# A hybrid diffusion backbone's mixers: ScalarE's background work behind the last traced eviction, longer runs of small matmuls, two-pass time steps

## The chip, the core and the metric

The kernel runs on one core of one Trainium2 chip. The metric is device time in microseconds (us), the median over runs. TensorE (PE in the rows) does the matmuls, VectorE (DVE) and ScalarE (ACT) the element-wise work; both of these read the matmul results from PSUM, which has eight banks.

## The reference

Two layers over 256 latent tokens and 256 context tokens of width 1024, in fp32. Each layer runs three token mixers on the same normalised input (a bidirectional state-space scan, "SSD", with a short convolution ahead of it; neighbourhood attention; a Conformer convolution of 31 taps), merges them by sigmoid gates, projects by `w_o`, and then runs a SwiGLU (dense in layer 0, a mixture of experts in layer 1).

```
def token_mixer(h_lat, h_ctx, lp, need_ctx):
    ...
    xs_l, bm_l, cm_l = ssd_prepare(h_lat @ w_xbc, lp['ssd_conv_w'], lp['ssd_conv_b'])
    ...
    y_lf, _ = ssd_direction(xs_l, bm_l, cm_l, h_lat @ w_dtf, a_log[0], dt_bias[0], st_f, False)
    ...
    ssd_l = ssd_output(y_lf, y_lb, xs_l, h_lat @ w_z, lp['ssd_d'], lp['ssd_norm'], lp['ssd_out'])
    ...
    na_l = na_latent(heads(h_lat @ w_q), heads(h_lat @ w_k), heads(h_lat @ w_v), k_c, v_c, lp['na_rpb']) @ lp['na_out']
    conf_l = conformer_branch(h_lat @ w_glu, lp['conf_conv_w'], lp['conf_conv_b'], lp['conf_ln_g'], lp['conf_ln_b'], lp['conf_out'])
    out_l = merge_branches(h_lat @ w_gate, (ssd_l, na_l, conf_l)) @ lp['w_o']
```

The SSD works in chunks of 128 tokens: `scores` of C and B, times a decay `exp` of differences of a running sum, times the inputs scaled by the time step `dt` (the within-chunk part), plus C times the incoming state, scaled by `exp(cs)` (the part across chunks). The shift, scale and gate of the norms (`ada`) are products of the conditioning vector with `ada_w`.

## The kernel before

**Projections.** `wstat` (weights stationary, L205 to L207) and `wmov` (L251 to L253) run all projections. Weights come in units of 512 KB. ScalarE rounds a unit to a high part `h_...` (L116), VectorE subtracts it from the raw values to get the low part `l_...` (L117), and each product is three matmuls: high by high, high by low, low by high. Each chunk of 512 output columns uses four of PSUM's banks ("acc"), and each bank is read out ("evicted") by ScalarE or VectorE when its sum is complete. The gates' evictions are sigmoids on ScalarE (`g<-wg`, L682), the short convolution's are copies into `uL` followed by five taps on VectorE (L572) and a SiLU (L560).

**Background work.** Beside the projections run jobs, written as Python generators: `att` (attention: scores `S` L750 and L770, softmax, transposes `PT` L740, values `po` L786), `ssd` (states `stS` L954, decay tiles `MS` by four Relus and an Exp on ScalarE, L1054 and L1055, then a product on VectorE, L1056; within-chunk sums `ydS` L1063; parts across chunks `yoS` L1080 scaled by `ES`, L1077), `conv` (31 taps on `ccv`, then a layer norm and a SiLU L830) and `ada` (sums `adac` on VectorE L374, then column sums on TensorE L382). `pump` is called behind each group of products and takes steps from every job until its credit is used; a step's `yield` is its price. Small matmuls are put off by one or two steps (`defer`), and `behind` ties them to the last large matmul written so far: on TensorE they stand behind it. They write to the other four banks of PSUM ("pw"). Other engines are not tied in this way: a scheduler sets the order on ScalarE and VectorE by priority, program order and what is ready.

**Order of the mixers.** Layer 0: `glu dt qkv xbc ssd g1 p1 g2 p2 z g0 p0`; layer 1 has `z` ahead of `p2`. `g1`, `g2`, `g0` are the gates, `p2` is the Conformer's projection (`wb0conf_out`), `p1` attention's (`wb0na_out`). The time steps are 24 matmuls of `wdtH` and `wdtL` with 32 columns each (L865 to L867) and four small transposes.

## Time and profile before

| | us |
|---|---|
| median of three runs (2364.26 to 2365.93) | 2364.38 |
| the profiled execution | 2367.87 |
| its span, from the first instruction to the last | 2366.1 |
| layer 0's mixers, about | 30 to 690 |
| the dense FFN | 690 to 1010 |
| layer 1's mixers, about | 1095 to 1515 |
| the experts | 1560 to 2366 |

Times in the rows are from the span's start. A row of the timeline gives start, length, engine, line, operation, output and inputs, tile shape, and how many records were merged; a matmul of plain fp32 leaves two records. Matmuls overlap in the pipeline, so the distance between two starts is what one costs, not its length. `128*64` is the shape of the part of the array that is used: two matmuls on different halves run together.

### The profile page before, as it was taken

To read this page: it belongs to the slowest core of one execution; us is meant where nothing else is said; L and a number is where in the kernel's file an instruction comes from. 1 tells how busy PE (TensorE), PEld (TensorE's weight loads), DVE (VectorE), ACT (ScalarE), POOL (GpSimd) and SP (SyncE) were. 2 spreads that over 40 slices of the span, in tenths; PEclk is the share of its full clock that TensorE was granted. 3 is DMA by queue.
4 is the path that set the end of the run, shared out by engine and by line. 5 is a ranking of instruction groups with operands and counts; after the bars stand their busy time and mean duration, and the time that the engine had idled before them with its cause. 6 is when DMAs were issued, how large, how long until landed. Compare 5 with 4: busy or idle time off the path is not lost.

```text
span 2366.1 us, 29723 instructions
## 1 busy us (share of the span) xinstructions
PE 2226.4 (94%) x11075; PEld 1632.5 (69%) x11075; DVE 1509.5 (64%) x2384; ACT 1030.1 (44%) x1658; POOL 17.4 (1%) x32
## 2 busy tenths in 40 slices
PE   7999999699999999999999889899999989999897
PEld 3776677477777777788877779766655656566564
DVE  3667999787667665536898765743433555565556
ACT  4334673643342222225347685443332345454453
POOL 0000000000000000000000000000000000000000
PEclk9999999899999999999999999999999999999998
DMA  7232253445445556423423344488888899999995
GB/s 269 95 117 72 76 172 127 116 156 169 147 143 160 173 175 199 147 98 102 147 89 104 107 146 161 139 324 330 341 320 320 330 365 375 357 385 347 348 370 206
DMA packets 123658, 492.51 MB, mean 208 GB/s; under 512 B 12784, under 2 KB 23792, under 8 KB 89712
## 3 DMA queue, kind: packets, MB, share of 16 engines
q1 hardware_dynamic: 122656, 487.89, 57.4%
q10 hardware_dynamic: 848, 2.62, 0.3%
q8 instruction: 89, 1.46, 0.2%
q14 instruction: 65, 0.53, 0.1%
HBM read 488.24 MB, written 2.23 MB: 207 GB/s over the span
## 4 chain that ended last, share of the span: by engine, by line
PE 71%; issue 11%; DVE 7%; DMA 6%; ACT 4%; POOL 0%; SPq 0%; POOLq 0%; DVEq 0%; ACTq 0%
PE er L1546 8%; PE nn L1428 7%; PE e L1546 4%; DMA adaw<-in_ada_w_dram 4%; PE ndn L1453 4%; PE edr L1546 3%; PE ed L1546 2%; PE wg L205 2%; PE wg L207 2%; PE wg L206 2%; DVE adac L374 2%; PE xbcL L205 1%; PE xbcL L206 1%; PE xbcL L207 1%; PE fu L206 1%
## 5 line engine op out<-in xcount | busy, mean ns | idle before, releaser
L374 DVE SCALAR_TENSOR_TENSOR adac<-adaw,sc,adac 128x512 f32<-128x512 f32 x224 | 160.1, 747 | 57.3 <-DMA adaw<-in_ada_w_dram 56.7
L117 DVE TENSOR_TENSOR l_er<-r_er,h_er 128x1024 fp32r<-128x1024 f32 x132 | 154.5, 1218 | 59.9 <-ACT h_er L116 59.5
L1428 PE MATMUL nn<-r_ngun,xn 128*64 128x512 f32 (+1 forms) x768 | 168.2, 561 | 0.0
L116 ACT ACTIVATE h_er<-r_er 128x1024 fp32r<-128x1024 f32 x132 | 133.0, 1053 | 42.2 <-DMA r_er<-in_moe_gu_dram 29.4
L205 PE MATMUL wg<-hHm,h_wg 128*128 128x512 f32 (+1 forms) x384 | 135.7, 355 | 1.8 <-ACT g L682 1.1
L206 PE MATMUL wg<-hLm,h_wg 128*128 128x512 f32 (+1 forms) x384 | 129.9, 339 | 0.0
L207 PE MATMUL wg<-hHm,l_wg 128*128 128x512 f32 (+1 forms) x384 | 128.8, 339 | 0.5 <-DVE l_wg L117 0.4
L1546 PE MATMUL er<-h_er,gHp 128*128 128x512 f32 (+1 forms) x288 | 110.5, 389 | 17.7 <-ACT h_er L116 17.7
L1428 PEld LDWEIGHTS nn<-r_ngun,xn 128*64 128x64 f32 x768 | 54.2, 137 | 91.9 <-issue 85.1
L1546 PE MATMUL er<-h_er,gLp 128*128 128x512 f32 (+1 forms) x288 | 108.1, 381 | 0.0
L117 DVE TENSOR_TENSOR l_e<-r_e,h_e 128x1024 fp32r<-128x1024 f32 x44 | 52.2, 1222 | 63.5 <-ACT h_e L116 62.6
L1453 PE MATMUL ndn<-r_ndn,hnn 128*64 128x512 f32 x352 | 87.4, 598 | 0.0
L572 DVE SCALAR_TENSOR_TENSOR ccv<-cu,cols,ccv 128x488 f32<-128x488 f32 (+14 forms) x120 | 84.5, 729 | 1.0
L1443 DVE TENSOR_TENSOR hnn<-npn,nsn 128x256 f32<-128x256 f32 (+1 forms) x24 | 9.6, 401 | 117.6 <-ACT nsn L1441 117.6
L1433 ACT ACTIVATE ntn<-nn 128x512 f32<-128x512 f32 (+1 forms) x24 | 13.5, 561 | 162.7 <-PE nn L1428 162.7
L1546 PE MATMUL er<-l_er,gHp 128*128 128x512 f32 (+1 forms) x288 | 84.3, 381 | 0.0
L205 PEld LDWEIGHTS wg<-hHm,h_wg 128*128 128x128 f32 x384 | 72.7, 189 | 14.5 <-issue 4.0
L1546 PEld LDWEIGHTS er<-h_er,gHp 128*128 128x128 f32 x288 | 54.8, 190 | 40.2 <-ACT h_er L116 29.0
L116 ACT ACTIVATE h_wg<-r_wg 128x1024 fp32r<-128x1024 f32 x48 | 50.6, 1058 | 71.8 <-PE wg L206 52.0
L117 DVE TENSOR_TENSOR l_edr<-r_edr,h_edr 128x1024 fp32r<-128x1024 f32 x66 | 77.0, 1217 | 4.4 <-ACT h_edr L116 4.1
L207 PEld LDWEIGHTS wg<-hHm,l_wg 128*128 128x128 f32 x384 | 72.2, 189 | 10.1 <-DVE l_wg L117 2.1
L206 PEld LDWEIGHTS wg<-hLm,h_wg 128*128 128x128 f32 x384 | 72.8, 190 | 8.8 <-issue 2.3
(642 smaller groups left out, 5955.5 us busy)
## 6 DMA issues: line engine op xcount, KB each, us to landing
r_ngun<-in_moe_gu_dram SPq DMA_DIRECT2D x88, 1024.0 KB, 7.1
r_er<-in_moe_gu_dram SPq DMA_DIRECT2D x66, 1024.0 KB, 7.3
r_ndn<-in_moe_down_dram SPq DMA_DIRECT2D x44, 1024.0 KB, 7.6
adaw<-in_ada_w_dram SPq DMA_DIRECT2D x160, 256.0 KB, 3.1
r_edr<-in_moe_down_dram SPq DMA_DIRECT2D x33, 1024.0 KB, 7.4
r_wg<-in_w_in_dram SPq DMA_DIRECT2D x48, 512.0 KB, 3.6
r_e<-in_moe_gu_dram SPq DMA_DIRECT2D x22, 1024.0 KB, 7.6
cbS<-csd SPq DMA_DIRECT2D x24, 512.0 KB, 4.9
```

The lines of the kernel that those rows point to most:

```text
L116: nc.scalar.activation(Hd, src, AF.Copy)
L117: nc.vector.tensor_tensor(Ld, src, Hd.bitcast(F32), op=ALU.subtract)
L205: mm(out, wh, xh, start=(first and kk == 0), stop=False, skip_group_check=True)
L206: mm(out, wh, xl, start=False, stop=False, skip_group_check=True)
L207: self.last = mm(out, wl, xh, start=False, stop=(kk == kc - 1), skip_group_check=True).ins
L374: nc.vector.scalar_tensor_tensor(d, w, c, d, op0=ALU.mult, op1=ALU.add)
L572: nc.vector.scalar_tensor_tensor(y[:, :, a:b], x[:, :, a + s:b + s], w[:, k:k + 1], y[:, :, a:b], op0=ALU.mult, op1=ALU.add)
L1428: mm(ps[64 * h:64 * h + 64, :n], x[kk], w[:, h, k, :], start=(kk == 0), stop=(kk == KD - 1), skip_group_check=True)
L1433: nc.scalar.activation(t, ps[:, :n], AF.Copy)
L1443: nc.vector.tensor_tensor(d, v[:, :, 1], g, op=ALU.mult)
L1453: mm(ps[64 * h:64 * h + 64], hT[:, kk * 64:(kk + 1) * 64], w[:, h, k, :], start=(kk == 0), stop=(kk == fc - 1), skip_group_check=True)
L1546: mm(ps[s][j], st[kk], w[p][:, k, :], start=(kk == 0 and p == 0 and q == 0), stop=(kk == kc - 1 and p == 1), skip_group_check=True)
```

## The change

1. `pump` and `drain` take every step of a background job under `evicted()`: what the step puts on the engine of the last eviction written so far stands behind that eviction. `note` keeps the last one; the evictions that return their instruction are ScalarE's.
2. Attention's two heads of a pair are turned together, for one or both query blocks at once, and the `po` matmuls wait in `joined` until the next turn. SSD's states of both directions run together; its within-chunk sums are one run of 8 matmuls per direction instead of two of 4, and the second direction's run also holds both `yoS` groups and the final sum.
3. The column sums of `ada` wait one more step and are tied behind the last large matmul; a step's price is 0.64 instead of 0.7.
4. conv5's SiLUs are put off by a chunk.
5. The time steps multiply by a tile that holds the high and low weights side by side (64 columns), and by the high one alone for the input's low part: 16 matmuls instead of 24. The transposes are 64 wide, and VectorE adds the two halves.

```diff
@@ -153,7 +154,7 @@
-                    with self.prio(job[3]):
+                    with self.prio(job[3]), self.evicted():
                         job[2] -= next(job[0])
...
+    def evicted(self):
+
+        return ExitStack() if self.lastev is None else self.tc.issue_after(self.lastev)
+
+    def note(self, r):
+        if r is not None:
+            self.lastev = r.ins
...
-                            evac(c * 4 + o, out)
+                            self.note(evac(c * 4 + o, out))
...
@@ -372,15 +382,17 @@
-                    yield 0.7 * len(streams)
+                    yield 0.64 * len(streams)
...
+            yield len(streams)
             ps = self.pw(f"ada{l}{g}{j0}")
-            for s in streams:
...
+            with self.behind():
+                for s in streams:
...
@@ -553,11 +565,15 @@
-            nc.scalar.activation(ut, ps, AF.Copy)
+            r = nc.scalar.activation(ut, ps, AF.Copy)
+        if len(self.silus) > 1:
+            self.silus.pop(0)()
...
-        nc.scalar.activation(ut, cvt[:, :ns * 256], AF.Silu)
+
+        self.silus.append(lambda: nc.scalar.activation(ut, cvt[:, :ns * 256], AF.Silu))
+        return r
...
@@ -728,19 +746,29 @@
-                def turn(P, j, qb, PT=PT, nm=nm, nk=nk, nkb=nkb, st=st):
-
-                    nc.vector.tensor_scalar(P, P, st[:, j, qb, 5:6], None, op0=ALU.mult)
+                def turn(P, qbs, PT=PT, nm=nm, nk=nk, nkb=nkb, st=st):
+
+                    for j in range(2):
+                        for qb in qbs:
+                            nc.vector.tensor_scalar(P[j][qb], P[j][qb], st[:, j, qb, 5:6], None, op0=ALU.mult)
...
+                        pts = [self.pw(f"PT{nm}{j}{qbs[0]}") for j in range(2)]
+                        n = len(qbs) * 128
+                        for f in joined:
+                            f()
+                        joined.clear()
...
+                    self.defer(q_, turned, 1)
...
-                        for j in range(2):
-                            turn(P[j], j, qb)
-                            yield 1.7
+                        turn([{qb: p} for p in P], (qb,))
+                        yield 3.4
...
-                self.defer(q_, values)
-                yield 0.5
+
+                self.defer(q_, lambda f=values: joined.append(f), 1)
...
@@ -855,27 +886,28 @@
-            nc.tensor.matmul(ps[0:32, :], wH[:, k, :], self.h[0][k], start=(k == 0), stop=False)
-            nc.tensor.matmul(ps[0:32, :], wH[:, k, :], self.h[1][k], start=False, stop=False)
-            nc.tensor.matmul(ps[0:32, :], wL[:, k, :], self.h[0][k], start=False, stop=(k == KD - 1))
+            nc.tensor.matmul(ps[0:64, :], wp[:, k, :], self.h[0][k], start=(k == 0), stop=False, skip_group_check=True)
+            nc.tensor.matmul(ps[0:32, :], wp[:, k, 0:32], self.h[1][k], start=False, stop=(k == KD - 1), skip_group_check=True)
...
-        nc.vector.tensor_tensor(b3(x), b3(pt[:, :n]), bc(self.col("dtb")), op=ALU.add)
+        pt = pt[:, :2 * n].rearrange("p (b q h) -> p b q h", b=NB, q=2)
+        nc.vector.tensor_tensor(b3(x), pt[:, :, 1], bc(self.col("dtb")), op=ALU.add)
+        nc.vector.tensor_tensor(b3(x), pt[:, :, 0], b3(x), op=ALU.add)
...
@@ -945,16 +977,19 @@
+                def state(g=g, xe=xe):
+                    ps = {r: self.pw(f"st{nm}{b}{r}{g}") for r in dirs}
+                    for r in dirs:
+                        nc.tensor.matmul(ps[r], Bp[:, g * 128:(g + 1) * 128], xe[r], start=True, stop=True)
...
@@ -1043,57 +1078,55 @@
-                    def diag(r=r, hq=hq, M=M, g=g, xd=xd, st=st):
...
-                    self.defer(q_, diag)
-                    yield 1.8
...
-                def off(r=r, g=g, E=E.rearrange("p i l -> p (i l)"), st=st):
-                    nc.scalar.activation(E, E, AF.Exp)
...
+                def diag(r=r, M=M, g=g, xd=xd, st=st, E=E):
...
+                    for e in E.values():
+                        nc.scalar.activation(e, e, AF.Exp)
+                    for hl in range(8):
+                        nc.tensor.matmul(st["pd"][64 * (hl % 2):64 * (hl % 2) + 64, (hl // 2) * 128:(hl // 2 + 1) * 128],
...
+                self.defer(q_, diag, 1)
+                yield 1.8 if r == 0 else 4.2
```

ScalarE ahead of layer 0's Conformer projection (`wb0conf_out`), before: the gate's evictions are `g<-wg`; `MS`, `ES` belong to the SSD, `ccv` and `c` to the Conformer.

```order
L1077 ACT_TABLE_LOAD
L1077 ACTIVATE ES_3614<-ES_3614 128x512
L1077 ACTIVATE ES_3638<-ES_3638 128x512
L116 ACTIVATE c_0_3305<-ccv_0_607 128x512
L830 ACT_TABLE_LOAD
L830 ACTIVATE ccv_2_608<-ccv_2_608,cols_60 128x512 x2
L116 ACTIVATE c_2_3306<-ccv_2_608 128x512
L682 ACT_TABLE_LOAD
L682 ACTIVATE g_4_2957<-wg_0_3288 128x512
L682 ACTIVATE g_4_2957<-wg_1_3289 128x512
L116 ACTIVATE c_2_3306<-ccv_2_608 128x512
L682 ACTIVATE g_6_2958<-wg_2_3290 128x512
```

The same place in the changed kernel:

```order
L1108 ACTIVATE ES_3368<-ES_3368 128x512
L117 ACTIVATE c_0_3286<-ccv_0_607 128x512
L861 ACT_TABLE_LOAD
L861 ACTIVATE ccv_0_607<-ccv_0_607,cols_60 128x512
L861 ACTIVATE ccv_2_608<-ccv_2_608,cols_60 128x512
L117 ACTIVATE c_0_3286<-ccv_0_607 128x512
L117 ACTIVATE c_2_3287<-ccv_2_608 128x512
L861 ACTIVATE ccv_2_608<-ccv_2_608,cols_60 128x512
L700 ACT_TABLE_LOAD
L700 ACTIVATE g_4_2933<-wg_0_3269 128x512
L700 ACTIVATE g_4_2933<-wg_1_3270 128x512
L1089 ACTIVATE MS_3521<-cbS_3437,cs_663 128x128 x4
```

In what is shown, the Conformer's last three SiLUs share one table load, and the two `ES` Exps that stood between them with a load of their own are gone from there.

TensorE in layer 0's attention, before, between large products (`L207`, `L205`): transposes `PT` and scores `S` mixed.

```order
L207 MATMUL wg_0_2169<-hHm_256,l_wg_0_2176 128x512
L740 MATMUL PT_1974<-con_t,P_1908 128x128 x2
L750 MATMUL S_1983<-kTL_2_703,qL_2_701 128x512
L740 MATMUL PT_1974<-con_t,P_1908 128x128
L750 MATMUL S_1984<-kTL_2_703,qL_2_701 128x512
L740 MATMUL PT_1974<-con_t,P_1908 128x128
L740 MATMUL PT_2004<-con_t,P_1909 128x128 x4
L205 MATMUL wg_0_2169<-hHm_256,h_wg_1_2255 128x512
L206 MATMUL wg_0_2169<-hLm_258,h_wg_1_2255 128x512
```

And a turn of the changed kernel, inside `xbc`:

```order
L216 MATMUL xbcL_3_1493<-hLm_259,h_xbcL_3_1727 128x512
L767 MATMUL PT_1585<-con_t,P_1519 128x128 x4
L767 MATMUL PT_1586<-con_t,P_1520 128x128 x4
L778 MATMUL S_1600<-kTL_0_694,qL_0_692 128x512
L778 MATMUL S_1601<-kTL_0_694,qL_0_692 128x512
L778 MATMUL S_1658<-kTL_0_694,qL_0_692 128x512
L778 MATMUL S_1659<-kTL_0_694,qL_0_692 128x512
L217 MATMUL xbcL_3_1493<-hHm_257,l_xbcL_3_1728 128x512
L813 MATMUL po_1684<-PT_1537,vL_0_696 64x256
```

All transposes of a turn stand first, then all four scores together; the values `po` stand in a run of their own behind one large matmul.

TensorE in layer 0's SSD beside a gate, before: a run of one quad, two products, and a run of `yoS`.

```order
L207 MATMUL wg_0_2430<-hHm_257,l_wg_2_2549 128x512
L1063 MATMUL ydS_2482<-MS_2507,xdS_2415 64x128 x4
L205 MATMUL wg_1_2431<-hHm_257,h_wg_2_2548 128x512
...
L207 MATMUL wg_1_2431<-hHm_257,l_wg_2_2549 128x512
L1080 MATMUL yoS_2588<-uL_10_1142,hsS0c_2187 128x128 x4
L205 MATMUL wg_2_2432<-hHm_257,h_wg_2_2548 128x512
```

After:

```order
L217 MATMUL wg_3_2405<-hHm_257,l_wg_2_2521 128x512
L1110 MATMUL ydS_2488<-MS_2451,xdS_2391 64x128 x4
L1110 MATMUL ydS_2488<-MS_2478,xdS_2391 64x128 x4
L1116 MATMUL yoS_2585<-uL_10_1134,hsS0c_2180 128x128 x4
L215 MATMUL wg_0_2402<-hHm_257,h_wg_3_2598 128x512
```

Both quads of a direction and the `yoS` group stand in one run.

## Rows read from the trace of the kernel before

**Rows 1.** The page: busy time by engine.
```profile
PE 2226.4 (94%) x11075; PEld 1632.5 (69%) x11075; DVE 1509.5 (64%) x2384; ACT 1030.1 (44%) x1658; POOL 17.4 (1%) x32
```

**Rows 2.** Busy time by stretch: length, five engines (instructions), TensorE's clock, DMA share, GB/s.
```profile
220.00:435.00 215.00, 214.66 (x1077) 157.17 (x1075) 197.81 (x357) 119.82 (x245) 1.05 (x1) 1.00 0.36 115
435.00:465.00 30.00, 9.75 (x71) 5.57 (x70) 21.43 (x37) 28.27 (x54) 0.00 (x0) 0.74 0.60 158
1380.00:1420.00 40.00, 32.55 (x241) 28.53 (x240) 20.99 (x32) 35.77 (x54) 0.00 (x0) 0.91 0.33 98
```

**Rows 3.** TensorE's timeline: a run of one quad and a run of two.
```profile
361.16 0.39 PE L207 MATMUL wb0na_out<-o0H,l_wb0na_out 128*128 128x512 f32 x1
361.48 0.66 PE L1063 MATMUL ydS<-MS,xdS 128*64 128x128 f32 x8
...
362.41 0.40 PE L206 MATMUL wb0na_out<-o0L,h_wb0na_out 128*128 128x512 f32 x1
...
488.66 0.39 PE L205 MATMUL wb0conf_out<-c,h_wb0conf_out 128*128 128x512 f32 x1
488.98 1.09 PE L1063 MATMUL ydS<-MS,xdS 128*64 128x128 f32 x16
...
490.34 0.40 PE L207 MATMUL wb0conf_out<-c,l_wb0conf_out 128*128 128x512 f32 x1
```

**Rows 4.** TensorE's timeline, 272 to 279 us: a lone score matmul, then two together.
```profile
272.25 1.12 PE L750 MATMUL S<-kTL,qL 64*128 64x512 f32 x2
273.30 0.33 PE L740 MATMUL PT<-con_t,P 128*128 128x128 f32 x1
...
277.93 1.13 PE L750 MATMUL S<-kTL,qL 64*128 64x512 f32 x4
278.99 0.50 PE L205 MATMUL wg<-hHm,h_wg 128*128 128x512 f32 x1
```

**Rows 5.** TensorE's timeline around layer 0's time steps.
```profile
89.83 0.39 PE L207 MATMUL gaL<-hHm,l_gaL 128*128 128x512 f32 x1
90.06 0.39 PE L865 MATMUL dt<-hHm,wdtH 128*32 128x512 f32 x1
...
95.38 0.39 PE L867 MATMUL dt<-hHm,wdtL 128*32 128x512 f32 x1
95.61 0.39 PE L205 MATMUL qL<-hHm,h_qL 128*128 128x512 f32 x1
```

**Rows 6.** Who TensorE waited for, 435 to 465 us: total, times, longest.
```profile
PE wb0conf_out L205 <- ACT g L682: 11.4, 1, 11.4
```

**Rows 7.** ScalarE's timeline, 435 to 468 us (cut).
```profile
435.12 1.06 ACT L116 ACTIVATE h_wb0conf_out<-r_wb0conf_out 128x1024 fp32r<-128x1024 f32 x1 [2.11 <-PE wg L206]
436.08 1.26 ACT L1054 ACTIVATE MS<-cbS,cs 128x128 f32<-128x128 f32 x4
437.25 0.62 ACT L1055 ACTIVATE MS<-MS 128x512 f32<-128x512 f32 x1
...
462.82 1.28 ACT L682 ACT_TABLE_LOAD   x1
464.12 1.09 ACT L682 ACTIVATE g<-wg 128x512 f32<-128x512 f32 x2
...
467.13 1.08 ACT L682 ACTIVATE g<-wg 128x512 f32<-128x512 f32 x2 [1.41 <-DVE cL L117]
```

**Rows 8.** ScalarE by line, 1380 to 1420 us: count, busy, mean ns, idle before.
```profile
L682 ACT ACT_TABLE_LOAD x7 | 9.0, 1283 | 0.1
```

**Rows 9.** Who TensorE waited for, 1380 to 1420 us.
```profile
PE ydS L1063 <- DVE MS L1056: 2.4, 2, 1.7
PE zL L205 <- ACT g L682: 1.7, 2, 1.5
```

**Rows 10.** Column sums of ada on TensorE, 690 to 1010 us.
```profile
L382 PE MATMUL ada<-adac,con_t 128*32 128x512 f32 x32 | 14.3, 600 | 7.2 <-DVE adac L374 7.0
```

**Rows 11.** VectorE's taps of the short convolution, 220 to 435 us.
```profile
L572 DVE SCALAR_TENSOR_TENSOR cvL<-uL,cols,cvL 128x508 f32<-128x508 f32 (+1 forms) x32 | 23.2, 742 | 0.0
```

More of the change, by code (lines that the diff above doesn't have):

```diff
@@ L59, in __init__ @@
         self.bg = []
-        self.last = None
+        self.last = self.lastev = None
+        self.silus = []
         ep = ctx.enter_context
@@ L189, in drain @@
                 self.bg.remove(job)
-                for _ in job[0]:
-                    pass
+                with self.evicted():
+                    for _ in job[0]:
+                        pass
     def wstat(self, wu, kc, cols, x, tok, evac, name, early=False):
@@ L619, in xbc @@
             self.wstat(W("xbc"), KD, 1536, h, xtok, lambda o, ps: self.conv5(o, ps, u, nm), "xbc" + nm)
+            while self.silus:
+                self.silus.pop(0)()
         def ssd():
@@ L721, in attention @@
         streams = ([(0, 256, False)] if l == 0 else []) + [(nt - 256, 512, True)]
-        q_ = []
+        q_, joined = [], []
         for q0, nk, lat in streams:
@@ L778, in attention @@
                         nc.vector.reciprocal(st[:, j, :, 5], st[:, j, :, 5])
-                        for qb in range(2):
-                            turn(P[j][:, qb * 256:(qb + 1) * 256], j, qb)
-                        yield 1.5
+                        yield 1.2
+                    turn([{qb: p[:, qb * 256:(qb + 1) * 256] for qb in range(2)} for p in P], (0, 1))
+                    yield 0.6
                 def values(hp=hp, PT=PT, nm=nm, nkb=nkb, q0=q0):
@@ L788, in values @@
                     self.split(po[:, 0:256], o_[0][hp][:, q0:q0 + 256], o_[1][hp][:, q0:q0 + 256])
-                self.defer(q_, values)
-                yield 0.5
+                self.defer(q_, lambda f=values: joined.append(f), 1)
         yield from self.undefer(q_)
+        yield 1.0
+        with self.behind():
+            for f in joined:
+                f()
     def conv31(self, cu, cv, nt):
@@ L1058, in diag @@
-                    def diag(r=r, hq=hq, M=M, g=g, xd=xd, st=st):
-                        if "pd" not in st:
-                            st["pd"] = self.pw(f"yd{nm}{b}{g}")
-                        for i in range(4):
-                            hl = hq * 4 + i
-                            nc.tensor.matmul(st["pd"][64 * (i % 2):64 * (i % 2) + 64, (hl // 2) * 128:(hl // 2 + 1) * 128],
-                                             xd[r][:, hl * 64:(hl + 1) * 64], M[:, i, :],
-                                             start=(r == 0 and hl < 2), stop=(r == 1 and hl > 5), skip_group_check=True)
@@ L1066, in ssd_y @@
-                    self.defer(q_, diag)
-                    yield 1.8
-            for r in range(2):
-                if hin[r] is None:
-                    continue
-                E = self.t2(f"E{nm}{b}{g}{r}").rearrange("p (i l) -> p i l", i=4)
-                for j in range(2):
-                    nc.sync.dma_start(E[64 * j:64 * j + 64], rows(r, g).rearrange("(i j) l -> j i l", j=2)[j][None].to_broadcast([64, 4, 128]))
-                def off(r=r, g=g, E=E.rearrange("p i l -> p (i l)"), st=st):
-                    nc.scalar.activation(E, E, AF.Exp)
-                    po = self.pw(f"yo{nm}{b}{g}{r}")
-                    for i in range(4):
-                        nc.tensor.matmul(po[:, i * 128:(i + 1) * 128], hin[r][:, g * 512 + i * 128:g * 512 + (i + 1) * 128],
-                                         u[10 + g][:, bs], start=True, stop=True)
-                    nc.vector.tensor_tensor(E, E, po, op=ALU.mult)
-                    if "prev" in st:
-                        nc.vector.tensor_tensor(E, E, st["prev"], op=ALU.add)
-                    st["prev"] = E
-                self.defer(q_, off)
-                yield 1.2
@@ new lines, in ssd_y @@
+                    nc.scalar.activation(m, m, AF.Exp, scale=-1.0)
+                    nc.vector.tensor_tensor(m, m, scm[:, r, g, None, :].to_broadcast([128, 4, 128]), op=ALU.mult)
+                    if hq == 0:
+                        yield 1.8
+                E = {}
+                for d in range(2) if r else ():
+                    if hin[d] is None:
+                        continue
+                    E[d] = self.t2(f"E{nm}{b}{g}{d}").rearrange("p (i l) -> p i l", i=4)
+                    for j in range(2):
+                        nc.sync.dma_start(E[d][64 * j:64 * j + 64], rows(d, g).rearrange("(i j) l -> j i l", j=2)[j][None].to_broadcast([64, 4, 128]))
@@ new lines, in diag @@
+                def diag(r=r, M=M, g=g, xd=xd, st=st, E=E):
+                    if r == 0:
+                        st["pd"] = self.pw(f"yd{nm}{b}{g}")
+                    E = {d: e.rearrange("p i l -> p (i l)") for d, e in E.items()}
+                    for e in E.values():
+                        nc.scalar.activation(e, e, AF.Exp)
+                    for hl in range(8):
+                        nc.tensor.matmul(st["pd"][64 * (hl % 2):64 * (hl % 2) + 64, (hl // 2) * 128:(hl // 2 + 1) * 128],
+                                         xd[r][:, hl * 64:(hl + 1) * 64], M[r, hl // 4][:, hl % 4, :],
+                                         start=(r == 0 and hl < 2), stop=(r == 1 and hl > 5), skip_group_check=True)
+                    po = {d: self.pw(f"yo{nm}{b}{g}{d}") for d in E}
+                    for d in E:
+                        for i in range(4):
+                            nc.tensor.matmul(po[d][:, i * 128:(i + 1) * 128], hin[d][:, g * 512 + i * 128:g * 512 + (i + 1) * 128],
+                                             u[10 + g][:, bs], start=True, stop=True)
+                    if r == 0:
+                        return
+                    prev = st["pd"]
+                    for d, e in E.items():
+                        nc.vector.tensor_tensor(e, e, po[d], op=ALU.mult)
+                        nc.vector.tensor_tensor(e, e, prev, op=ALU.add)
+                        prev = e
+                    for i in range(4):
+                        y = u[g * 4 + i][:, bs]
+                        nc.vector.scalar_tensor_tensor(y, y, self.col("dsk", g * 4 + i), prev[:, i * 128:(i + 1) * 128], op0=ALU.mult, op1=ALU.add)
```

69 lines of the change are left out of this document (30 added, 39 removed).

## The prediction

> **What bounds the kernel now.** I read the busy times first. TensorE is busy for 94% of the span [rows 1]: whatever does not shorten TensorE's own stream, or one of the few holes in it, moves nothing. The second view is busy time by stretch. From 220 to 435 us TensorE has no hole (214.66 of 215 us), and VectorE beside it is busy for 197.81 us, 92%; from 435 to 465 us TensorE works for only 9.75 of 30 us while ScalarE works for 28.27; from 1380 to 1420 us it works for 32.55 of 40 while ScalarE works for 35.77 [rows 2]. So there are two kinds of time to win: small matmuls inside a full TensorE stream, and two stretches where ScalarE ends last. The waits and ScalarE's timeline say why: the first conformer projection waits 11.4 us for the gate's eviction [rows 6], which starts at 464.12 us, 29 us after the weight copy at 435.12, behind background SSD and conformer work [rows 7].
>
> The sum is made against the profiled execution, 2367.87 us (span 2366.1 and 1.8 around it); that is 3.5 us above the median of 2364.38, and I carry the difference over to the median.
>
> **Longer small runs: price of a run.** [Rows 3] show one group of four `ydS` matmuls (8 records) between large ones. From the start of the large matmul ahead (361.16) to the second large one behind (362.41) it is 1.25 us; two large matmuls alone take 2 x 0.23 (their pitch, [rows 5]: 89.83 to 90.06), so the run costs 0.79. Two groups together (16 records) cost 488.66 to 490.34, 1.68 less 0.46, or 1.22. The second group adds 0.43; the first one's work is then also 0.43, and the other 0.36 is entering and leaving: about 0.18 for each change of tile shape. Full-shape small ones (`PT`, `yoS`, `stS`) pay no such charge, so joining those alone wins nothing. A score matmul that stands alone has a second price. In [rows 4] a lone one (x2) takes 272.25 to 273.30, 1.05 us; two for the two halves of the array (x4) take 277.93 to 278.99, 1.06. A lone one wastes the slot of its pair: 0.87 of 512 columns, 0.44 of 256.
>
> Counted over the whole order of TensorE up to the end of layer 1's mixers, changes of tile shape fall from 215 to 161: 54 x 0.18 = 9.9 us. Slots of the array's two halves fall by five for scores of 512 columns, 5 x 0.87 = 4.4; by three for scores of 256, 3 x 0.44 = 1.3; by three for `po`, also of 256, 1.3; and by one for `ada`, of 512, 0.87. The number of `ydS` slots stays. Together **-17.7 us**, of which -15.6 lie in layer 0 up to the end of gate 2, +1.4 behind it (ada runs moved there), -2.8 in `w_o` and the dense FFN, -0.6 in layer 1.
>
> **What VectorE takes back.** About 10.3 of the 15.6 us fall between 220 and 435 us, where VectorE has only 17.2 us idle in 215 [rows 2]. A stretch of 205 us would leave it 7. Its work stays nearly the same (the taps, the splits of the weights, the scalings), and TensorE cannot run ahead of the splits. The bounds are 0 and 10.3; I take **+5**, the middle, since no row shows which side of 7 us it needs.
>
> **ScalarE's background behind the last eviction.** In [rows 7] the order ahead of the first gate-2 eviction after the copy at 435.12 is 27 Relus, seven Exps of `MS`, four of `ES`, four SiLUs, three copies and six table loads. In the changed order there are 19 Relus, five and two Exps, four SiLUs, three copies, four table loads. So 8 Relus x 0.3 (four take 1.26), 4 Exps x 0.6 (one takes 0.62), and 2 loads x 1.28 [rows 7]: 2.4 + 2.4 + 2.6 = 7.4. The evictions still write the buffers that the conformer's SiLU outputs leave, and wait for VectorE's split of them (the second pair did, 1.41 us [rows 7]), so some may stay: I take **-6.5**, with 2 and 10 as ends. Next late behind it is the same projection's own operand, made by the same SiLUs.
>
> A table load costs 1.28 us and the next instruction starts 1.30 after it (462.82 to 464.12 [rows 7]); nothing else is lost. The Trainium skill ("ScalarE: Activation LUTs", What ACT_TABLE_LOAD costs) adds a drain of about 1.38 us to each switch; by it the two loads would give 2.8 us more. The trace shows no drain.
>
> In layer 1 the evictions of the last gate stand one by one between table loads: seven loads for `g` alone in 40 us [rows 8]. The changed order has three of the last four in a row, and 8 loads of all kinds in the stretch where 12 stood. TensorE's hole there is 7.45 us [rows 2], of which 1.7 are `zL` waiting for these evictions and 2.4 `ydS` waiting for `MS`, both behind the same crowded ScalarE [rows 9]. Four loads are 5.1 us; the ends are 0 and the whole hole, and I take **-4**, these two waits.
>
> What is queued behind: the SSD's Exps come later, and `ydS` waits for them on TensorE. This is the price named as the slower rival below.
>
> **Row sums of ada put off.** In the FFN TensorE waits 7.2 us ahead of 32 records of `ada` [rows 10]. The first two groups of the changed order are joined and stand behind large matmuls, eight stay single: I take **-1**. Three more now stand in layer 0 behind gate 2. At most each waits for VectorE as these do: 32 records are 16 matmuls, or 0.45 of the 7.2 for each matmul and 0.9 for a pair; I take half, 3 x 0.5 = **+1.5**; ends 0 and 3.
>
> **Two-pass time steps.** 24 matmuls become 16 in each layer; one is 0.23 us [rows 5], so 8 x 0.228 x 2 = **-3.6**. The new pairs alternate 64 and 32 stationary columns. [Rows 5] show that going from a full 128 columns to 32 costs 0.23, the plain pitch, and back the same. The Trainium skill ("TensorEngine Tiling (Array Packing)", Key Properties) speaks against it: changing the tiling mode drains TensorE. [Rows 3] agree for `ydS`, [rows 5] do not for `dt`; I follow the row of the same matmul. Ends -3.6 and +1.8 (the third rival). The two more VectorE additions are small and early.
>
> **Parts at nothing.** conv5's SiLU put off by one chunk: it stands behind the next chunk's copy instead of ahead of it, and what reads it is the SSD's background work, later; if it were late, that work waits and not the projections. The joined `turn` and `values` do the same VectorE work.
>
> **The sum.** -17.7 + 5 - 6.5 - 4 - 1 + 1.5 - 3.6 = -26.3: 2341.6 for the profiled execution, **2338** on the median.
>
> **The rivals.** (1) *VectorE or the order takes back all of layer 0's runs.* If VectorE is the bound there, the 15.6 are lost instead of 5: 2349. For: the 92%. Against: TensorE lost 0.34 us in those 215 us.
> (2) *The change doesn't bring the evictions forward.* They are still behind 19 Relus and four loads, and behind VectorE's split; then neither -6.5 nor -4 comes: 2349.
> (3) *The alternating shapes of dt pay the 0.18.* 15 more changes x 0.18 less 1.8 is +0.9 in each layer instead of -1.8: 2343.5. The page named above is this rule.
> (4) *Slower.* A joined run takes two or three of the four work banks of PSUM at once, and TensorE's queue is in order: a run whose banks are not yet read, or whose scaling is not yet done, stops the large matmuls behind it. VectorE reads them between taps: a group of five is 5 x 0.742 [rows 11] = 3.7 us, so a run meets it for 1.9 us on average. About 20 joined runs stand in layer 0: 20 x 1.9 = 38, 2376. It decides from 1.3 us a run (no gain left), 1.55 to be slower by more than can be measured. Against: single runs on the same banks lost nothing between 220 and 435 us. (5) *The same at about 1.3 us a run*: nothing is left to measure, 2364.
>
> **How the numbers follow.** Forecast 0.50; (1) 0.10; (2) 0.13; (3) 0.12; (5) 0.08; (4) 0.07. A difference of 0.2% is about what a measurement of this kernel can tell from none. Faster: 0.50 + 0.10 + 0.13 + 0.12 = 0.85; same 0.08; slower 0.07. The range holds the forecast and the first three rivals, and leaves out (4) and (5). The low end: VectorE takes nothing back, -10 in place of -6.5, -7.5 in place of -4, ada at no cost: 2364.4 - 17.7 - 10 - 7.5 - 1 - 3.6 is 2325. The high end: VectorE takes 10.3, -2 and 0 from ScalarE, the time steps cost 1.8 and ada 1.5: 2364.4 - 17.7 + 10.3 - 2 + 1.5 + 1.8 is 2358.
>
> **What would show it.** Right: 435 to 465 us shortened to some 23 us with the wait for `g` at 5 or less; `ydS` x16 runs at 1.22, `S` x4 at 1.06; 220 to 435 shorter by 5; 16 `dt` records at a 0.23 pitch; fewer table loads at 1380 to 1420. Wrong: TensorE waits for `PT`, `P` or `MS` at many joined runs in layer 0, VectorE above 97% there, `dt` at 0.4 a step.

## The result, and the profile after

The changed kernel took 2332.9 us (median of four runs, 2323.26 to 2336.53) where before took 2364.32; the ratio is 0.9862, 95% interval 0.9829 to 0.9894. Forecast were 2338 and a range of 2325 to 2358. Timed a second time beside the experiments it took 2328.07 against 2360.88, ratio 0.9855 (0.9836 to 0.9874). So it is faster by 31 to 34 us, and the forecast of 26 was short by 5 to 8.

The page of the changed kernel has TensorE at the same share of a shorter span, which answers to [rows 1]:

```profile
span 2334.8 us, 29702 instructions
...
PE 2201.5 (94%) x11059; PEld 1625.4 (70%) x11059; DVE 1510.4 (65%) x2382; ACT 1035.4 (44%) x1658; POOL 17.4 (1%) x32
```

The busy times of three stretches (length, then TensorE, its weight loads, VectorE, ScalarE, GpSimd, TensorE's clock, DMA share, GB/s). The first is the work from `xbc` to the middle of attention's projection; the second, from the last weight copy ahead of the Conformer's projection to its start, answers to [rows 2], 435 to 465; the third is the first quarter of `z` in layer 1, the end of 1380 to 1420 there:

```profile
161.00:342.10 181.10, 177.19 (x906) 130.46 (x905) 166.07 (x324) 119.11 (x250) 0.00 (x0) 1.00 0.32 106
420.90:441.80 20.90, 7.54 (x71) 5.47 (x69) 13.49 (x23) 20.74 (x40) 0.00 (x0) 0.78 0.49 152
1376.80:1385.20 8.40, 7.20 (x56) 6.58 (x55) 5.62 (x7) 7.17 (x8) 0.00 (x0) 1.00 0.24 80
```

The same work before, cut at the same products:

```profile
165.20:355.60 190.40, 190.14 (x905) 132.84 (x904) 161.91 (x317) 115.73 (x250) 0.00 (x0) 1.00 0.33 105
435.00:464.80 29.80, 9.55 (x71) 5.37 (x69) 21.23 (x37) 28.07 (x54) 0.00 (x0) 0.74 0.60 159
1401.50:1418.40 16.90, 12.54 (x80) 10.25 (x80) 10.19 (x19) 14.87 (x24) 0.00 (x0) 0.80 0.22 64
```

The first stretch went from 190.4 to 181.1 us. TensorE's busy time in it fell by 13.0 (190.14 to 177.19), and holes of 3.9 in all opened that were not there. The second went from 29.8 to 20.9, the third from 16.9 to 8.4. Who TensorE waited for in the changed kernel, first in 161 to 395 us, then in 420 to 442 (total, times, longest), and one more line of before, 435 to 465:

```profile
PE po L813 <- ACT P L786: 2.9, 3, 1.0
PE wg L215 <- ACT h_wg L117: 1.0, 1, 1.0
```

```profile
PE ydS L1110 <- DVE MS L1091: 7.8, 4, 3.3
PE wb0conf_out L215 <- ACT g L700: 5.6, 1, 5.6
```

```profile
PE ydS L1063 <- DVE MS L1056: 8.9, 3, 3.9
```

In the new holes TensorE waits for ScalarE, not for VectorE. Three runs of `po` wait about 1 us each for line 786, the Exp that reads scores out of PSUM and writes nothing that `po` reads; so by the code they wait for a bank. The fourth, 1.0 us, is a gate's product waiting for its rounded weights `h_wg`. The wait of [rows 6] went from 11.4 to 5.6, and that of `ydS` beside it only from 8.9 to 7.8. ScalarE's timeline around that eviction, to be set against [rows 7]: it starts 20.2 us behind the copy (420.94 to 441.14) instead of 29.0.

```profile
420.94 1.06 ACT L117 ACTIVATE h_wb0conf_out<-r_wb0conf_out 128x1024 fp32r<-128x1024 f32 x1 [4.32 <-PE wg L216]
...
439.85 1.28 ACT L700 ACT_TABLE_LOAD   x1
441.14 1.09 ACT L700 ACTIVATE g<-wg 128x512 f32<-128x512 f32 x2
```

The time steps on TensorE's timeline, against [rows 5], with the first products behind them:

```profile
87.45 0.39 PE L217 MATMUL gaL<-hHm,l_gaL 128*128 128x512 f32 x1
87.68 0.39 PE L896 MATMUL dt<-hHm,wdtp 128*64 128x512 f32 x1
87.91 0.39 PE L897 MATMUL dt<-hLm,wdtp 128*32 128x512 f32 x1
...
91.14 0.40 PE L897 MATMUL dt<-hLm,wdtp 128*32 128x512 f32 x1
91.37 0.40 PE L215 MATMUL qL<-hHm,h_qL 128*128 128x512 f32 x1
```

Sixteen steps take 87.68 to 91.37, 3.69 us, or 0.23 each: 64 and 32 columns alternate at the plain pitch.

**Stage by stage.** The order of the 5808 records of large products is nearly the same in all kernels here, so the start of the record with the same number can be compared. The table has, for one profiled execution each, how much longer or shorter than before a stage took from its first product to the next stage's, in us (worked out from TensorE's timelines; the column "before" has lengths).

| stage | before | after | again (e9) | e1 | e2 | e3 | e4 | e6 |
|---|---|---|---|---|---|---|---|---|
| layer 0 up to `xbc` | 135.8 | -3.9 | -2.3 | -1.1 | -1.8 | -1.2 | -3.7 | -1.8 |
| `xbc`, gate 1, `p1`, most of gate 2 | 245.4 | -10.9 | -11.0 | -1.4 | -7.9 | -3.5 | -11.1 | -0.1 |
| end of gate 2 to the Conformer's projection | 54.1 | -7.8 | -7.8 | -6.6 | -0.3 | +1.1 | -0.5 | +0.2 |
| that, `z`, gate 0, `ssd_out` | 189.7 | +0.4 | +0.3 | +4.8 | +0.7 | -2.6 | -0.9 | +4.1 |
| `w_o`, dense FFN | 449.5 | -5.9 | -11.2 | -0.4 | -1.2 | -1.3 | -10.9 | -8.2 |
| layer 1 up to gate 1 | 183.5 | -2.2 | -1.3 | -2.0 | -1.9 | -1.1 | -0.8 | -0.8 |
| gate 1, `p1`, gate 2 | 114.0 | +6.0 | +5.4 | -2.8 | +3.7 | +3.3 | +1.7 | +1.0 |
| `z` | 32.9 | -8.5 | -6.8 | 0.0 | 0.0 | -8.5 | -8.5 | 0.0 |
| the rest of layer 1's mixers | 90.7 | +1.2 | -1.8 | -1.7 | -0.1 | +1.7 | -2.4 | -0.9 |

e1, e2, e3 and e6 are the kernel before with one part; e4 is the changed kernel without one. Differences of up to some 5 us in a row can come from TensorE's granted clock alone, as the last section shows.

### The profile page after: what moved, and what is told of

It is laid out like the page before. It is cut to its first block, busy times and chain, and to the rows that moved or that the text cites. A ratio compares the mean times of both kernels' runs of the same rounds, so it can differ in the third digit from the quotient of the medians.

```text
span 2334.8 us, 29702 instructions
## 1 busy us (share of the span) xinstructions
PE 2201.5 (94%) x11059; PEld 1625.4 (70%) x11059; DVE 1510.4 (65%) x2382; ACT 1035.4 (44%) x1658; POOL 17.4 (1%) x32
## 4 chain that ended last, share of the span: by engine, by line
PE 70%; issue 10%; DVE 9%; DMA 5%; ACT 5%; POOL 0%; SPq 0%; POOLq 0%; DVEq 0%; ACTq 0%
PE er L1579 8%; PE nn L1461 7%; PE e L1579 4%; PE edr L1579 4%; PE ndn L1486 3%; DMA adaw<-in_ada_w_dram 3%; PE ed L1579 2%; PE wg L215 2%; PE wg L217 2%; PE wg L216 2%; DVE ccv L588 2%; PE fu L216 1%; PE fu L215 1%; PE fg L216 1%; PE fu L217 1%
```

## The experiments

Unless a time is called one of the profile, ratios are to before on the same chip, with 95% intervals.

The kernels did not run at the same granted clock. Here are the mean of the recorded clocks over a kernel's executions, the same for before beside it, and the difference of the median times:

| run | its clock | clock of before | us against before |
|---|---|---|---|
| e1 | 0.9831 | 0.9804 | -6.1 |
| e2 | 0.9789 | 0.9804 | -3.1 |
| e3 | 0.9806 | 0.9804 | -9.2 |
| e4 | 0.9792 | 0.9804 | -23.9 |
| e5 | 0.9800 | 0.9805 | +6.5 |
| e6 | 0.9792 | 0.9805 | +0.6 |
| e9, the changed kernel | 0.9825 | 0.9794 | -32.8 |
| e10 | 0.9810 | 0.9794 | -32.9 |
| e11 | 0.9800 | 0.9794 | -20.3 |
| e12 | 0.9838 | 0.9794 | -31.0 |

Among the 25 executions of before beside e1 the shortest, 2355.22 us, had 0.983 and the longest, 2368.68, had 0.977. By these two, 0.003 goes with some 7 us in one and the same kernel (an estimate). So a difference of a few us between two kernels whose clocks differ by 0.002 or 0.003 does not show what an edit is worth by itself. The clock can't simply be subtracted either: part of it is lost in holes where TensorE waits anyway (0.74 in the second stretch above), and an edit that shortens a hole may change the clock with it.

**e1: the background behind the evictions, alone.** The edit is `evicted`, `note` and their calls, and no other hunk:

```diff
-                    with self.prio(job[3]):
+                    with self.prio(job[3]), self.evicted():
...
-                            evac(c * 4 + o, out)
+                            self.note(evac(c * 4 + o, out))
```

> The kernel before with part 1 alone: background steps stand behind the last eviction; nothing else is changed. Theory (the terms of the sum add up, each part acts by itself): in ScalarE's order between the weight copy ahead of the Conformer projection and the first gate-2 eviction 26.0 us of work become 17.7 us, so that the eviction starts about 20.5 us behind that copy instead of 29.0; in layer 1 the gate and z stretch (1361 to 1418 us before) shortens by about 4; TensorE's runs cost 1.2 more. In all -9 to -11, about 2354. Rival A (most of the 31 us comes from this part, the longer runs give back what they win): -20 or more, 2344 or less. Rival B (the order alone wins nothing, since what stands behind the eviction is waited for by the next TensorE run): within 3 of before, with the hole only moved.

Measured: 0.9970 (0.9957 to 0.9984), -7 us by the ratio. The eviction starts 22.4 us behind the copy, of which ScalarE waits 1.95 for VectorE's split `cL`:

```profile
433.11 1.06 ACT L117 ACTIVATE h_wb0conf_out<-r_wb0conf_out 128x1024 fp32r<-128x1024 f32 x1 [1.65 <-PE wg L216]
...
455.47 0.60 ACT L693 ACTIVATE g<-wg 128x512 f32<-128x512 f32 x1 [1.95 <-DVE cL L118]
```

The stage wins 6.6 us, and the fourth row of the table gives back 4.8. `z` of layer 1 wins nothing: its first quarter takes 16.9 us as before, at a clock of 0.90 instead of 0.80. Rival A falls; the theory holds at the Conformer's projection and fails for `z`. Rival B, a hole that is only moved, is not excluded: in layer 0 the trace keeps 1.8 of the 6.6 us, attention's projection in layer 1 takes 28.7 us at a clock of 1.00 instead of 32.6 at 0.90, and the clock of the timed executions is 0.0027 above that of before, which by the estimate above is about as much as the 6 to 7 us. What this part alone is worth in time stays open.

**e2: attention's joined turns, alone.** The hunks of `attention`, nothing else:

```diff
-                        for j in range(2):
-                            turn(P[j], j, qb)
-                            yield 1.7
+                        turn([{qb: p} for p in P], (qb,))
+                        yield 3.4
...
-                self.defer(q_, values)
+                self.defer(q_, lambda f=values: joined.append(f), 1)
```

> The kernel before with attention's joined turns and values alone. Theory: by the order, tile shape changes and slots cost TensorE 11.2 us less, 11.3 of it in layer 0 up to the end of gate 2; in layer 0 about 3 us come back as waits of the po runs for a PSUM bank that ScalarE still reads (three of 0.97 in the changed kernel), and in layer 1 about 6 as waits of joined transposes for VectorE's scaling. In all -2 to -3, about 2362; layer 0 alone -8. Rival A: nothing left in layer 0 either (VectorE bound there), 0 there and +6 in layer 1: 2370. Rival B: the waits come from other parts and not from joining, -11: 2353.

Measured: 0.9980 (0.9969 to 0.9992), -5 us. Layer 0 wins 7.9 in the second row, with the waits of `po` (2.7 us) and of `wg` (1.0) that the changed kernel has; e12 below, which has all but this part, has neither. Layer 1's gate 1 loses 3.8, where transposes wait 6.3 us for VectorE instead of 3.2 (first this kernel, then before):

```profile
PE PT L749 <- DVE P L735: 5.0, 2, 3.3
PE PT L749 <- DVE st L767: 1.3, 1, 1.3
```

```profile
PE PT L740 <- DVE P L733: 3.2, 1, 3.2
```

So the theory holds in both places. The joining also makes the steps of a pair of heads cheaper by 0.5 in the prices of `yield`; what that does by itself was not tried.

**e3: the SSD's joined runs, alone.**

```diff
-                    self.defer(q_, diag)
-                    yield 1.8
...
+                self.defer(q_, diag, 1)
+                yield 1.8 if r == 0 else 4.2
```

> The kernel before with the SSD's joined states and joined within-chunk runs alone. Theory: by the order TensorE's runs cost 3.2 us less, but ScalarE now has 31.6 us of work instead of 26.0 ahead of the first gate-2 eviction, since the background stands ahead of it: -3 from runs, +5.6 at the Conformer projection, in all about +2, 2366 to 2367. Rival A (each run joined pays, whatever the eviction): -3 or better, 2361. Rival B (the second direction's run waits for all four tiles of MS at every block): +8 or more, with waits of ydS for MS in all eight blocks, 2372.

Measured: 0.9955 (0.9943 to 0.9968), -11 us. That is rival A's time (-3 or better), but no expectation had the place where it is won. ScalarE's extra work came as counted (the eviction 33.8 us behind its copy), but the copy itself came earlier, so the stage lost only 1.1; and `z` of layer 1 won 8.5. Its first quarter in this kernel, to be set against the row of before above:

```profile
1355.30:1396.30 41.00, 37.67 (x333) 34.34 (x332) 27.23 (x45) 36.88 (x68) 0.00 (x0) 1.00 0.54 166
1396.30:1404.70 8.40, 7.20 (x56) 6.59 (x55) 5.65 (x7) 7.15 (x8) 0.00 (x0) 1.00 0.22 75
```

This part, and not the eviction's order, carries `z`. In before, e1, e2, e6 and e11 the first quarter of `z` holds 24 records of `ydS` and eight Relus of `MS` (by the timelines); in e3 and in every kernel with this part it holds none.

**e4: the changed kernel with part 1 undone.**

```diff
-                    with self.prio(job[3]), self.evicted():
+                    with self.prio(job[3]):
```

> The changed kernel with part 1 undone (background steps no longer behind the last eviction), all else kept. Theory: ScalarE's work ahead of the first gate-2 eviction goes from 18.9 to 26.0 us, so the Conformer projection starts 7 us later against its weight copy; layer 1's gate and z stretch loses 4: about +11, 2344. Rival A (this part carries most of the gain): +20 or more, 2353 or above. Rival B (the longer runs do without it): within 3 of the changed kernel.

Measured: 0.9895 (0.9870 to 0.9921), 0.0040 or 9 us more than e9's 0.9855, near the 11 expected, though the two intervals overlap by a hair (another chip) and the profiled execution of e4, with a span of 2331.0, is no longer than e9's by that much (2328.0). The executions of e4 also had a clock of 0.979 and those of e9 0.9825, so the 9 us are not shown to be part 1's. The eviction is 27.5 us behind its copy again, and TensorE waits for it 12.9 us:

```profile
PE wb0conf_out L214 <- ACT g L699: 12.9, 1, 12.9
```

`z` of layer 1 keeps its -8.5, so the 4 us expected there did not come, and gate 1 of layer 1 is 4 us shorter than in the changed kernel: there part 1 costs. In the table's sums e4 and e9 are within 1 us of each other.

**e5: only the price of the SSD's steps.** e3 cheapens a block's steps from 10.8 to 9.6; here that is done without joining anything:

```diff
             self.defer(q_, fin)
-            yield 1.2
```

> The kernel before with one number changed: the last step of each SSD block and group has the price 0 instead of 1.2, so that the job's sum per block is 9.6, as in the changed kernel, instead of 10.8. No run is joined. Theory (layer 1's z stretch gained 8.5 us in the run with the SSD part alone because the job's steps are cheaper there, so that the SSD ends inside gate 2 and leaves z to the projection): the first half of z in layer 1 (16.9 us before) shortens by 7 to 9 here too; layer 0 loses: by the order runs cost 4 more up to gate 2, and 34.5 us of ScalarE's work stand ahead of the first gate-2 eviction instead of 26.0, +8; in all about +3, 2363 to 2368 beside a before of 2360 to 2364. Rival (the joined runs themselves did it): z in layer 1 is unchanged within 1.5, and the whole is +10 or more.

Measured: 1.0034 (1.0022 to 1.0046), +8 us where about +3 was expected. `z` of layer 1 wins 8.9 here too, so the price does end the SSD ahead of `z`. But gate 2 ahead of it loses 9.3:

```profile
1357.40:1407.50 50.10, 41.27 (x356) 37.61 (x355) 30.82 (x52) 43.80 (x79) 0.00 (x0) 0.93 0.49 147
1407.50:1415.50 8.00, 8.00 (x55) 8.00 (x55) 3.84 (x5) 5.87 (x7) 0.00 (x0) 0.79 0.50 161
```

```profile
PE ydS L1063 <- DVE MS L1056: 8.5, 4, 5.1
```

The price alone moves the stall. In e3 gate 2 takes 41.0 us and holds less of the SSD: 80 records of `ydS` and 32 Relus instead of 96 and 38 (by the timelines), since attention's projection ahead of it has taken 32 records of `ydS` instead of 16. ScalarE's table loads there and in the first quarter of `z` are 13 before ([rows 8] are seven of them) and 10 in e3:

```profile
L682 ACT ACT_TABLE_LOAD x5 | 6.4, 1283 | 0.1
...
L1058 ACT ACT_TABLE_LOAD x3 | 3.8, 1283 | 0.1
...
L1076 ACT ACT_TABLE_LOAD x2 | 2.6, 1283 | 0.0
```

So the cheaper steps are not enough; the gain came with them and the joined form together, whose `ES` Exps stand beside those of `MS`. The joined form at the old price was not tried.

**e6: ada's part alone.**

```diff
-                    yield 0.7 * len(streams)
+                    yield 0.64 * len(streams)
...
+            yield len(streams)
             ps = self.pw(f"ada{l}{g}{j0}")
...
+            with self.behind():
```

> The kernel before with ada's part alone (column sums one step later, tied behind the last large matmul, price 0.64). Theory (the dense FFN's first half shortened by 9 to 10 us in the two kernels that hold this part, and by nothing in the three that don't): -9 in the first half of the FFN, +1 to +3 in the second, +1.5 in layer 0 behind gate 2, in all -5 to -7, about 2355. Rival A (as the prediction had it): -1.4 from runs and -1 of waits, -2 to -3 in all. Rival B (the FFN's gain came with a luckier clock): the FFN within 2 of before at the same granted clock.

Measured: 0.9996 (0.9983 to 1.0010), so the theory's -5 to -7 did not come. The profile has -8.2 in `w_o` and the FFN and +4.1 behind gate 2. The FFN's gain is in the traces: up to its first down-projection it takes 95 to 97 us in every kernel with this part and 104 to 108 in every one without, and the waits of `ada` for VectorE are 3.5 here instead of 7.2 [rows 10]. It is not shown in the times, where e6 also had the lower clock, 0.979 against 0.9805.

```profile
L384 PE MATMUL ada<-adac,con_t 128*32 128x512 f32 x32 | 12.2, 601 | 3.5 <-DVE adac L374 3.4
```

**e7 and e10: the background behind the evictions in layer 0's mixers alone**, one kernel on two chips:

```diff
-        return ExitStack() if self.lastev is None else self.tc.issue_after(self.lastev)
+        return ExitStack() if self.lastev is None or not self.ev0 else self.tc.issue_after(self.lastev)
...
+        self.ev0 = l == 0
```

> The changed kernel with the background behind the evictions in layer 0's mixers alone, and free in the dense FFN and in layer 1. Theory (part 1 wins 7 at layer 0's Conformer projection and costs about 4 in layer 1, where attention's scaling on VectorE waits for Exps that stand behind evictions, and transposes on TensorE wait for it): layer 0 as in the changed kernel, gate 1 and gate 2 of layer 1 shorter by 4; in all -4, or 7 less than with part 1 undone: 2326 to 2330. Rival A (part 1 wins in layer 1 what it costs there): the same as the changed kernel within 2. Rival B (part 1 wins in layer 1): +3 or more.

> The kernel of e7 (background behind the evictions in layer 0's mixers alone) beside the changed kernel on one chip. Theory: in layer 1's gate 1 it is 4 to 5 us shorter, everything else equal, so 4 to 6 us faster than the changed kernel, about 0.002 of the ratio. Rival (what e7's profile showed is given back elsewhere or was its clock): within 1.5 us of the changed kernel.

e7 gave 0.9858 (0.9826 to 0.9891), e10 0.9859 (0.9839 to 0.9879). On one chip e10's 2328.03 stands beside e9's 2328.07: no difference, as the rival had it, though e10's clock was the lower one (0.981 against 0.9825). In the traces gate 1 of layer 1 does shorten, from 45.8 and 45.3 us (the changed kernel's two profiles) to 41.4 and 42.5, because transposes wait less for the scaled `P`. TensorE's waits in that stage, in the changed kernel and in e10:

```profile
PE PT L767 <- DVE P L753: 7.0, 3, 4.1
```

```profile
PE PT L770 <- DVE P L756: 3.8, 1, 3.8
```

So the cost of part 1 in layer 1 is there in the traces, some 3 us, and does not show in the time. No kernel here that does all the work is measurably faster than the changed one.

**e8: shorter taps.**

```diff
-                self.taps(v(cu[i]), v(cv[i]), w[:, i], self.col("fb", i), (k,))
+                (self.taps(v(cu[i]), v(cv[i]), w[:, i], self.col("fb", i), (k,)) if l or k == CK // 2 else self.stap(v(cu[i]), v(cv[i]), w[:, i], k))
```

> The changed kernel with 30 of the 31 taps of layer 0's long convolution cut to 16 of 512 columns: the instructions stay, VectorE loses some 80 us of work between 60 and 410 us, and the convolution's result is left out. Theory (the runs' gain between 161 and 395 us was given back by waits for PSUM banks that ScalarE reads, three of 0.97 and one of 0.97, and not by VectorE): the time from xbc to the end of gate 1 stays within 2 us of the changed kernel, and the waits of po for ScalarE are still there. Rival (VectorE was the bound that took back the gain): that stretch shortens by 4 or more and the waits of po go. The Conformer's later steps come earlier, so what follows from gate 2 on is not compared.

This kernel leaves out most of layer 0's long convolution. Measured in its one execution: `xbc` to the middle of `p1` took 180.8 us against 181.1, and the waits of `po` were there:

```profile
163.60:344.40 180.80, 176.87 (x905) 130.51 (x905) 158.09 (x357) 115.53 (x245) 0.00 (x0) 1.00 0.30 105
```

```profile
PE po L813 <- ACT P L786: 3.5, 3, 1.4
```

That is the theory's side, but weaker than meant: other background work filled VectorE, which fell only from 166.07 to 158.09 us in that stretch, and moved within it (`xbc` alone took 105.4 us against 97.8, gate 1 less). Stronger is that TensorE has no wait for VectorE between 161 and 395 us in the changed kernel's own trace.

**e9, e11, e12: the changed kernel again, and without one of the two joinings.** e11 undoes the SSD's hunks, e12 attention's.

> The changed kernel itself, timed again beside the three others of this group, since the comparison with e7 needs one chip. Theory: the ratio to before stays at 0.986 within 0.003, and stage by stage the profile repeats the first one within 1 us, except where TensorE's granted clock is below 1 in one of the two. Rival (the first ratio was a lucky chip): 0.990 or more.

> The changed kernel with the SSD's joined states and within-chunk runs undone. Theory (the SSD part carries z of layer 1, and layer 0's runs beside gate 1, gate 2 and z): z in layer 1 +8.5, layer 0 +1.8 +1.6 +2.8, ScalarE's work ahead of the first gate-2 eviction 16.6 instead of 18.9, -2: about +12, 2345. Rival (the part overlaps with the others): +5 or less.

> The changed kernel with attention's joined turns and values undone. Theory: layer 0's xbc stretch loses its 7.6, ScalarE's work ahead of the first gate-2 eviction is 22.2 instead of 18.9, +3; layer 1's gate 1 wins 4 to 5 since fewer transposes wait for VectorE's scaling: about +6, 2339. Rival A (the joined turns are worth more in company): +10 or more. Rival B (they are worth nothing): within 2.

Measured on one chip: e9 2328.07; e11 2340.60, ratio 0.9905 (0.9879 to 0.9932), +12.5 as expected, with `z` of layer 1 back at its old length; e12 2329.85, ratio 0.9872 (0.9848 to 0.9896), +1.8. In the traces attention's joining is worth 6 in layer 0 (the second row of the table is -4.9 in e12) and costs about 3 in layer 1 (+2.6 in gate 1 to gate 2 instead of +5.4), which leaves some 3. The time is that of rival B of that run, but the clocks of the three differ (e9 0.9825, e11 0.980, e12 0.984): by the estimate above, e11's 12.5 would be too large for the SSD's part and e12's 1.8 too small for attention's.

## Why the prediction came out as it did

**Longer runs and VectorE (-17.7 and +5).** The second row of the table, -10.9 and -11.0, is near what the two terms gave for layer 0 up to the end of gate 2 (-15.6 + 5 = -10.6). The traces have the 54 changes of shape fewer (of which 54 x 0.18 is 9.7 us, not 9.9). The price of a run held to the hundredth: 372.24 to 373.92 is 1.68, less two products 1.22.

```profile
372.24 0.39 PE L217 MATMUL wg<-hHm,l_wg 128*128 128x512 f32 x1
372.56 1.09 PE L1110 MATMUL ydS<-MS,xdS 128*64 128x128 f32 x16
373.58 0.50 PE L215 MATMUL wg<-hHm,h_wg 128*128 128x512 f32 x1
373.92 0.40 PE L216 MATMUL wg<-hLm,h_wg 128*128 128x512 f32 x1
```

But the step behind the +5 failed: it was given to VectorE, and what came back are 3.9 us of waits for ScalarE, 2.9 of them at PSUM banks. That is the fourth rival's mechanism, at three places of about 1 us each. They come with attention's joining: e2 and e11 have them, e12 has none. That the +5 was near in size is luck.

**The eviction ahead of the Conformer's projection (-6.5).** Measured -7.8 for the stage; e1 has -6.6 from this part alone, e4 loses 7.3 without it. Here the mechanism is shown, for this stage; for the whole kernel e1 and e4 leave open what it is worth. Counting ScalarE's instructions between two points of the order (Relu 0.30, Exp and copy 0.52, SiLU 0.72, table load 1.29 us, all from starts in the trace of before) was a good measure of the time from the weight copy to the eviction in every kernel:

| kernel | counted, us | copy to eviction, us |
|---|---|---|
| e11 | 16.6 | 18.8 |
| e1 | 17.7 | 22.4 |
| changed | 18.9 | 20.2 |
| e12 | 22.2 | 24.0 |
| before | 26.0 | 29.0 |
| e4 | 26.0 | 27.5 |
| e3 | 31.6 | 33.8 |
| e5 | 34.5 | 37.0 |

**Layer 1's `z` (-4).** This step failed. The sum gave it to the order of evictions; e1, which has that order, wins nothing there, and e3, which hasn't, wins 8.5. What ended last in `z` was the SSD's tail, and it is gone since the cheaper and joined SSD ends inside gate 2 (e3, e11; e5 by the price alone). The clock is not the reason: e1 has the old length at 0.90, before at 0.80. The SSD's part was in the sum for its runs alone, and it moved the end of a whole job across a stage border; the prices in the `yield`s were not in the sum at all.

**What was not in the sum: +6 in layer 1's gates 1 and 2.** Joined transposes wait in gate 1 for scaled `P`, 7.0 us instead of 3.2. It takes attention's joining: e12, without it, has +0.9 in that gate, the changed kernel +5.1 and e2, the joining alone, +3.8. It is not always there with the joining: e4, with the old eviction order, has +0.9. Some of the 5.1 is the clock, 0.89 in that gate instead of 0.96. The slower rival named this mechanism and put it in layer 0; it came in layer 1, and it was paid by the SSD's unforeseen gain, which is luck.

**ada (-2.8 and -1 in the FFN, +1.4 and +1.5 behind gate 2).** Behind gate 2 e6 has +4.1 where 2.9 stood; in `w_o` and the FFN -6 to -11 where -3.8 stood. Two terms are mis-sized: the wait for VectorE, 7.2 us before, 2.7 in the changed kernel and 3.5 in e6, so -4 instead of -1; and the work, since TensorE's busy time in the FFN up to its first down-projection fell from 99.14 to 93.58 us at the same clock (0.98), 5.6 instead of 2.8. In the changed kernel the rows behind gate 2 keep only +0.4; e3, with the SSD's part alone, has -2.6 there.

```profile
L394 PE MATMUL ada<-adac,con_t 128*32 128x512 f32 x32 | 13.1, 630 | 2.7 <-DVE adac L384 2.6
```

**Time steps (-3.6).** Measured -1.9 in layer 0 (27.30 to 25.45 us for the stage from `gaL` to `qL`), and 16 steps at 0.23. In layer 1 the same stage takes 15.6 us at a clock of 1.00, and 17.4 in e1, e2 and e5, which have the old steps and that clock: -1.8. The third rival falls for this matmul: 64 and 32 columns alternate 15 times at the plain pitch. The Trainium skill ("TensorEngine Tiling (Array Packing)", Key Properties) says that changing the tiling mode drains TensorE; no drain shows in these 16 steps.

**The total.** By the rows of the table the forecast is -1.8, -10.6, -6.5, +2.9, -3.8, -1.8, -0.6, -4 and 0, together -26. The first profile is 5.4 us below it, the second 10.2. The largest misses are `z` (-4.5 in the first profile), the FFN and `w_o` (-2.1 and -7.4), the row behind gate 2 (-2.5) and, the other way, gates 1 and 2 of layer 1 (+6.6). That the total came so near is in part luck, since these misses have opposite signs. How much of the 5 to 8 us lies in the terms is open too: the timed executions of e9 had a clock 0.003 above that of before, which by the estimate above is as much.

The parts don't add up simply: alone they are worth 7, 5, 11 and 0 by the times, and the time steps 3.7 by the traces, together 27 of 31 to 34, with the clocks as they were. What stays open is which pairs make the rest, what the clock made of it, and what the conv5 SiLUs put off by a chunk are worth, which no kernel here tried alone.

## What to carry to other kernels

Where background work shares engines with evictions, count the instructions that the order puts on the engine ahead of an eviction: that count times the durations of the trace gave the time from the last weight copy to the eviction within 5 us in eight kernels. The prices by which a pump paces its jobs are part of a change, since a job that ends one stage earlier moves a stall of 8 to 9 us, for better (e3) or to another place (e5). Before a difference of a few us is put down to an edit, compare the granted clocks of the timed executions. And joining small matmuls into longer runs takes several PSUM banks at once: look for the engine that still reads them.

## What the runs showed of the hardware

TensorE's granted clock makes stages of the same work differ. Layer 1's stage from `gaL` to `qL`, in which TensorE has no hole, took 18.9 us at a mean clock of 0.91 (before) and 17.4 at 1.00 (e1), in kernels that have the same order there. The second half of the dense FFN in the changed kernel's two profiles:

```profile
778.00:926.40 148.40, 144.57 (x606) 110.89 (x605) 94.37 (x128) 35.69 (x43) 0.00 (x0) 0.98 0.60 191
```

```profile
778.60:922.10 143.50, 141.54 (x606) 109.46 (x606) 92.67 (x125) 34.83 (x41) 0.00 (x0) 1.00 0.58 193
```

The same products took 148.4 us at a mean granted clock of 0.98 and 143.5 at 1.00 (that is, at 2.4 GHz throughout). About 3 of the 4.9 us are the clock (0.02 of 148.4); the rest is waits, 3.8 us of holes instead of 2.0. The 0.98 is one stretch of 6.8 us at 1.2 GHz, which began while TensorE waited 2.6 us for `adac`. With another one earlier in the FFN it makes 10.2 us at 1.2 GHz; half of that is 5.1, and the fifth row of the table differs by 5.3 between the two profiles:

```profile
698.80:702.20 3.40, 3.40 (x18) 3.40 (x18) 2.45 (x4) 0.00 (x0) 0.00 (x0) 0.51 0.41 139
910.50:917.30 6.80, 6.33 (x13) 3.71 (x14) 3.47 (x5) 1.06 (x1) 0.00 (x0) 0.50 0.47 148
```

The other rows in which these two profiles differ by more than 1 us fit too: they differ by 1.6, 1.7 and 3.0, and half of the difference in time at 1.2 GHz is 1.7, 1.7 and 3.4. So a few us of one stage in one profile are no evidence without the clock beside them, and the forecast had no term for it. A shape change that by the estimate from [rows 3] costs 0.18 us for plain fp32 matmuls costs nothing for the time steps, whose operands are by the code rounded to fp32r; which of type, column offset or size makes the difference wasn't tried.
